# A hybrid decoder step on one core: state loads, weight splits, broadcast loads and a second half's operands in another order

## The chip, the core and the metric

The kernel runs on one core of a Trainium2 chip. The metric is device time in microseconds (us), from the start of the execution to its end; smaller is better. Engines are named as in the profile: PE is TensorE's matmul, DVE is VectorE, ACT is ScalarE, POOL is GpSimd, SP is SyncE, which here only issues DMAs.

## The reference

One layer of a decoder (model width 1024) for two groups that share the weights: a prompt of 1024 tokens and 8 samples of one token each, with carried states. All is float32.

```python
h = rmsnorm(x) * (1 + scale1) + shift1            # shift, scale, gate from the conditioning c
qkv, gate, beta, a, sq, sk, sv, ga, gb = split(h @ w_in)
y_a = (gated_rmsnorm(gated_delta_rule(conv4(qkv), beta, a)) ) @ w_gdn_out   # 8 heads, 128 x 128 state
y_b = sliding_window_attention_with_sinks(sq, sk, sv) @ w_swa_out
x   = x + gate1 * ((sigmoid(ga) * y_a + sigmoid(gb) * y_b) @ w_o)
h2  = rmsnorm(x) * (1 + scale2) + shift2
x   = x + gate2 * ((silu(causal_dwconv3(h2 @ w_ffn_gate)) * (h2 @ w_ffn_up)) @ w_ffn_down)
y   = rmsnorm(x)                                  # outputs: y and the new states of both groups
```

For the samples the delta rule is one step from a carried state S (8 samples, 8 heads, 128 x 128 floats: 512 KB a head): S' = exp(g) S + k delta, which is an output.

## The kernel before, in words

Every matmul operand in float32 is split in two parts of a shorter type: `split` (L127) lets ACT write the high part (`hi`, the page's L129) and DVE the low part `x - hi` (L130). A product is then three matmuls, hi hi, hi lo, lo hi (`mm3`, the page's L200, L201, L202). Tokens (1024 of the prompt and 8 samples) lie on the free axis in three `PARTS` of 384, 384 and 264; a weight of 1024 x 128 (512 KB) is loaded into `raw` and split into `wh` and `wl` by `load_split` (L147), which leaves the load in `self.w_load` and its two split instructions in `self.rounded`. `project_steps` (L167) gives 8 steps of three matmuls for one weight and one part.

What stands where in an engine's row is decided by a scheduler that simulates a timeline with priorities. `weave` (L1286) mixes several streams of steps by priority; `issue_after` says after which instruction another one is issued; `order(later, first)` (L132) puts instructions behind others of the same engine, without a wait. Each engine works its row in order, SP too: where a load waits for its buffer, all loads behind it wait.

The first half ends so:
- `delta_scan` (L946) runs the delta rule's chunks of the last head one after the other. A chunk is a chain of small steps: PE `rc` (L971), DVE `y` (L972), PE `rc` (L974), ACT `s` (L976), PE `rc` (L978), DVE the next `S` (L990). The last head's small DVE and ACT steps are kept in `self.small`, with the number of PE steps (`self.steps`) that had been recorded. `spaced` and `passed` (L181, L189) use them to spread the projections' matmuls and evictions between them: one PE step for every `self.every` = 2 projection steps, counted in `self.at`.
- `early_out` (L1332) is such a projection: the attention's output `ob` (kept in DRAM, laid in SBUF for parts 2 and 0) times the eight column blocks of `w_swa_out`, in `EARLY_ORDER` 0, 1, 2, 5, 6, 7, 3, 4; part 2 for all, part 0 also for blocks 3 and 4. Each result (`mm`) is multiplied by its gate tile (`gt`, loaded from `sgb` at L1353 into one of a few buffers) and goes to DRAM as `ub`. Here too the first six heads' sample states are loaded (`load_state`, L1144) into `b1h` and `b1l`.
- `branches` (L1363) does the rest of that product (part 1, loaded from `ob` into `b2l` in four quarters of 384 KB at L1278, and what is left of part 0), with the samples' delta rule (`sample_delta`, L1148) beside it, and then `y_a`: the delta rule's output `oa` times `w_gdn_out`, two blocks at a time. At the end of `sample_delta` each head's `delta` (in DRAM, `dlr`) is loaded as a broadcast into one of two halves of `db` (L1241, a `b1l` in the trace) and scaled with k by eight ACT instructions (L1243, `self.scaled`), then DVE forms the new state and POOL stores it.

The second half (`second_half`, L1959) is output projection, second norm and the FFN. `operands` (L1560) makes, of a half `p` of the tokens, seven combined operands (`ops[0]` to `ops[6]`, sums and differences of four quarters of x1), each split in hi and lo; stage 0 makes the first two, stage 1 the other five. For p = 1 their buffers are `bmh2, bml2, pk2, pk3, pk4, pk5, bmh3`. `pair_weights` (L1616) does the same to the FFN's weights (`w`, `ws`), and `ffn_gate_up` (L1693) runs the seven products of a pair (`wv`, `mm`, `wy` are their PSUM tiles) and recombines them on DVE and ACT.

Of the kernel before, what the change touches and what calls it, by code (L numbers as in the profile page):

```python
# [18 lines left out]
P = 128  # L19
NP = 1024  # L20
NS = 8
NT = NP + NS
KC = 8
H = 8
# [5 lines left out]
EARLY = (3, 4)  # L30
# [34 lines left out]
class Step:  # L65
# [1082 lines left out]
    def sample_delta(self, pool2):  # L1148

        nc, I = self.nc, self.I  # L1150
# [69 lines left out]
        dlr = self.t(self.dr, [H, NS, P], "dlr")  # L1220
# [16 lines left out]
        for h in range(H):  # L1237
            if h % 4 == 0:
                yield
            d = db[:, h % 2 * NP:h % 2 * NP + NP].rearrange("p (b v) -> p b v", b=NS)  # L1240
            nc.sync.dma_start(d, dlr[h].unsqueeze(0).broadcast_to([P, NS, P]))  # L1241
            for b in range(NS):
                made = nc.scalar.activation(d[:, b, :], d[:, b, :], AF.Copy, scale=kq[:, h, b, 0:1])  # L1243
                self.scaled.setdefault(h, []).append(made)
                nc.vector.scalar_tensor_tensor(S0[h][:, b, :], S0[h][:, b, :], self.egb[:, b, 0, h:h + 1], d[:, b, :],
                                               op0=ALU.mult, op1=ALU.add)
            nc.gpsimd.dma_start(self.O[3][0][:, h].rearrange("b k v -> k b v"), S0[h])
# [84 lines left out]
    def early_out(self):  # L1332

        nc = self.nc
        self.ubd = {t: self.t(self.dr, [8, P, PARTS[t][1]], f"ub{t}") for t in (2, 0)}
        load = lambda j: self.load_w(self.I["w_swa_out"][0][:, j * P:(j + 1) * P],
                                     where=self.fill_where[j % len(self.fill_where)])
        self.S0, states = [], [self.flat_room(self.b1, "b1", x, 1) for x in "hl"]
        X = {2: self.load_part(self.b1, self.ob, 2, "b1")}
        w = load(EARLY_ORDER[0])  # L1340
        for i, j in enumerate(EARLY_ORDER):
            if i == 3:
                self.obX = {0: self.load_part(self.b1, self.ob, 0, "b1")}
                X.update(self.obX)
            now, w = w, load(EARLY_ORDER[i + 1]) if i < 7 else None
            if i == 6:
                with self.tc.issue_after(self.w_load.ins):
                    for h in range(6):
                        self.load_state(h, states[h // 3])
            for t in (2, 0) if j in EARLY else (2,):  # L1350
                lo, n = PARTS[t]
                s = self.t(self.gt[0], [P, 384], self.gt[1])[:, :n]
                nc.sync.dma_start(s, self.sgb[j][:, lo:lo + n])  # L1353

                def out(t, ps):
                    with self.passed():
                        nc.vector.tensor_tensor(s, ps, s, op=ALU.mult)
                    nc.gpsimd.dma_start(self.ubd[t][j], s)

                for _ in self.project_steps(now, X, out, (t,), self.fill_psum):  # L1360
                    yield

    def branches(self, pool, pool2):  # L1363
        nc, I = self.nc, self.I
        first = self.part_rooms(pool2, 0)
        ob = {**self.obX, 1: self.load_part(pool2, self.ob, 1)}
        ub = [self.t(pool, [P, KC, n], f"t{t}", bufs=1) for t, (_, n) in enumerate(PARTS)]
        samples, rows, self.scaled = self.sample_delta(pool2), self.last_rows(), {}
        gate = lambda src, j, t: self.gate_part(pool if src is self.sga and j > 5 else self.gt[0], src[j][:, PARTS[t][0]:PARTS[t][0] + PARTS[t][1]], t)

        def yb_out(t, ps):
# [41 lines left out]
        for j0 in (0, 2, 4, 6):  # L1413
            w = []
            for j in (j0, j0 + 1):
                w.append(self.load_w(I["w_gdn_out"][0][:, j * P:(j + 1) * P]))
                for h in {1: range(3, H), 2: (6, 7)}.get(j, ()):
                    self.order(self.scaled[h], self.rounded)
            if 0 < j0 < 6:
                for j in (j0, j0 + 1):  # L1420
                    self.project(w[j - j0], oa, ya_out)
                continue

            for ts in ((0,), (2,), (1,)) if j0 == 0 else ((0,), (1,), (2,)):
                for j in (j0, j0 + 1):
                    self.project(w[j - j0], oa, ya_out, ts)
# [133 lines left out]
    def operands(self, pool, p, stage):  # L1560

        n = QUARTERS[2 * p][1]
        x1 = self.x1[p]
        a1, a2, b1, b2 = (x1[:, k:k + 4, c:c + n] for c in (0, n) for k in (0, 4))
        if stage == 0:
            self.X[p] = [(t[:, 0:4, :n], t[:, 4:8, :n]) for t in self.pair_tiles(p)]
        ops = self.X[p]
        if stage == 0:  # L1570
            self.split(*ops[0], a1)
            yield
            self.split(*ops[1], a2)
            yield
            return
        d = self.t(pool, [P, 4, QW], "td", bufs=1)[:, :, :n]
        minus = lambda out, x, y: self.nc.vector.tensor_tensor(out, x, y, op=ALU.subtract)
        minus(a1, b1, a1)
        self.split(*ops[3], a1)
        yield  # L1580
        minus(d, b2, a1)
        self.split(*ops[2], d)
        yield
        minus(b1, b2, b1)
        self.split(*ops[4], b1)
        yield
        minus(a2, a2, d)
        self.split(*ops[5], a2)
        yield
        self.split(*ops[6], b2)  # L1590
        yield


# [533 lines left out]
```

## Time and profile before

| | us |
|---|---|
| three runs | 2075.91, 2066.82, 2076.16 |
| their median | 2075.91 |
| profiled execution | 2069.76 |
| its span, first to last instruction | 2068.1 |
| PE busy | 2009.2 |
| DVE, ACT, POOL busy | 1356.6, 901.7, 525.0 |

The span is what the trace covers; the profiled execution is 1.7 us longer. Its mean granted TensorE clock is 0.990 of full speed. Times in the trace are counted from the span's start.

### The profile page before, as it was taken

The page shows a single profiled execution, that of the slowest core. Times are in us where ns is not written, and L with a number is a line of the kernel's source. Part 1 is how long each engine was busy: PE and PEld are TensorE (multiplying, and loading weights), DVE is VectorE, ACT ScalarE, POOL GpSimd, SP SyncE. Part 2 cuts the span into 40 slices and gives each one's busy share as a digit, 9 for nine tenths or more (in the row PEclk, how much of TensorE's full clock was granted, in tenths as well). Part 3 has the DMA queues.
Part 4 walks back from the last instruction along what each step waited for, and adds up shares of the span by engine and source line. Part 5 has one row for each costly group of instructions (what it writes and reads, how often), then busy time and mean ns, then how long its engine had stood idle before and what let it go on. Part 6 is the DMA issues. An engine that isn't in the chain of part 4 may idle for free.

```text
span 2068.1 us, 41309 instructions
## 1 busy us (share of the span) xinstructions
PE 2009.2 (97%) x16245; PEld 1909.6 (92%) x16245; DVE 1356.6 (66%) x2714; ACT 901.7 (44%) x2233; POOL 525.0 (25%) x604
## 2 busy tenths in 40 slices
PE   7999998999999999989999999999999999999998
PEld 4987877799999999989989999999999999999998
DVE  5755767483655746646554575579876777679876
ACT  4664545443344343442442352345544444445444
POOL 2000000121321211201112010104556556543551
PEclk9999999999999999989999999999999999999999
DMA  9256443332322322312248774522333333377783
GB/s 303 62 145 211 137 168 117 100 98 63 83 82 57 78 70 52 92 37 61 64 144 243 233 242 115 174 67 89 98 98 100 111 93 93 124 277 279 265 281 129
DMA packets 300960, 275.75 MB, mean 133 GB/s; under 512 B 59731, under 2 KB 246832, under 8 KB 300749
## 3 DMA queue, kind: packets, MB, share of 16 engines
q1 hardware_dynamic: 294202, 250.66, 39.7%
q0 software_dynamic: 6064, 21.85, 3.0%
q8 instruction: 127, 2.08, 0.4%
q14 instruction: 69, 0.56, 0.1%
q10 hardware_dynamic: 498, 0.61, 0.1%
HBM read 212.93 MB, written 62.51 MB: 133 GB/s over the span
## 4 chain that ended last, share of the span: by engine, by line
PE 85%; DVE 6%; DMA 4%; ACT 3%; issue 1%; SPq 0%; POOL 0%; ACTq 0%; DVEq 0%; POOLq 0%
PE mm L200 19%; PE mm L201 18%; PE mm L202 18%; PE wv L200 3%; PE wv L202 3%; PE wv L201 3%; PE wy L202 2%; PE wy L200 2%; PE wy L201 2%; PE pv L672 1%; DMA raw<-in_w_swa_out_dram 1%; PE pt L210 1%; PE tp L210 1%; PE mm L284 1%; PE rc L978 1%
## 5 line engine op out<-in xcount | busy, mean ns | idle before, releaser
L200 PE MATMUL mm<-b1h,wh 128*128 128x384 f32 (+1 forms) x1520 | 498.1, 329 | 3.4 <-ACT gt L1322 1.6
L201 PE MATMUL mm<-b1l,wh 128*128 128x384 f32 (+1 forms) x1520 | 489.9, 323 | 0.0
L202 PE MATMUL mm<-b1h,wl 128*128 128x384 f32 (+1 forms) x1520 | 488.6, 324 | 0.0
L200 PEld LDWEIGHTS mm<-b1h,wh 128*128 128x128 f32 x1520 | 287.6, 189 | 12.0 <-issue 4.6
L201 PEld LDWEIGHTS mm<-b1l,wh 128*128 128x128 f32 x1520 | 287.6, 189 | 4.4 <-issue 3.1
L202 PEld LDWEIGHTS mm<-b1h,wl 128*128 128x128 f32 x1520 | 286.6, 189 | 3.7 <-issue 2.8
L130 DVE TENSOR_TENSOR wl<-raw,wh 128x1024 fp32r<-128x1024 f32 x82 | 102.6, 1252 | 65.9 <-ACT wh L129 63.7
L129 ACT ACTIVATE wh<-raw 128x1024 fp32r<-128x1024 f32 x83 | 87.1, 1049 | 131.1 <-PE mm L201 80.0
L201 PE MATMUL mm<-pk,w 128*128 128x260 f32 (+1 forms) x440 | 124.7, 284 | 1.1 <-DVE pk L130 1.1
L200 PE MATMUL mm<-pk,w 128*128 128x260 f32 (+1 forms) x440 | 124.7, 284 | 0.0
L202 PE MATMUL mm<-pk,w 128*128 128x260 f32 (+1 forms) x440 | 124.5, 283 | 0.0
L130 DVE TENSOR_TENSOR w<-ws,w 128x512 fp32r<-128x512 f32 x88 | 78.8, 896 | 38.9 <-ACT w L129 38.7
L1666 ACT COPY bml<-mm 128x256 f32<-128x256 f32 (+1 forms) x132 | 49.0, 371 | 102.0 <-PE mm L202 99.4
L200 PE MATMUL mm<-bmh,w 128*128 128x260 f32 (+1 forms) x320 | 90.3, 282 | 0.0
L202 PE MATMUL mm<-bmh,w 128*128 128x260 f32 (+1 forms) x320 | 90.2, 282 | 0.0
L200 PE MATMUL mm<-b2h,wh 128*128 128x384 f32 (+1 forms) x256 | 83.3, 327 | 2.6 <-ACT wh L129 2.6
L1721 DVE SCALAR_TENSOR_TENSOR fa<-fz,fcw,fa 128x512 f32<-128x512 f32 x88 | 73.3, 854 | 18.4 <-ACT fa L1719 18.1
L201 PEld LDWEIGHTS mm<-pk,w 128*128 128x128 f32 x440 | 83.2, 189 | 1.3 <-DVE pk L130 1.3
L201 PE MATMUL mm<-b2l,wh 128*128 128x384 f32 (+1 forms) x256 | 83.6, 327 | 0.0
L200 PEld LDWEIGHTS mm<-pk,w 128*128 128x128 f32 x440 | 83.2, 189 | 0.2 <-ACT bml L1666 0.2
L202 PEld LDWEIGHTS mm<-pk,w 128*128 128x128 f32 x440 | 83.4, 190 | 0.0
L202 PE MATMUL mm<-b2h,wl 128*128 128x384 f32 (+1 forms) x256 | 82.6, 325 | 0.0
(648 smaller groups left out, 5886.7 us busy)
## 6 DMA issues: line engine op xcount, KB each, us to landing
raw<-in_w_in_dram SPq DMA_DIRECT2D x59, 512.0 KB
ws<-in_w_ffn_down_dram SPq DMA_DIRECT2D x55, 256.0 KB
raw<-xd SPq DMA_DIRECT2D x47, 258.0 KB
raw<-in_w_ffn_down_dram SPq DMA_DIRECT2D x47, 256.0 KB
raw<-in_w_ffn_gate_dram SPq DMA_DIRECT2D x22, 512.0 KB
raw<-in_w_ffn_up_dram SPq DMA_DIRECT2D x22, 512.0 KB
qst<-in_w_mod_dram SPq DMA_DIRECT2D x16, 512.0 KB
raw<-in_w_mod_dram SPq DMA_DIRECT2D x16, 512.0 KB
```

The source lines that it names most:

```text
L129: return (self.nc.scalar.activation(hi, x, AF.Copy), (eng or self.nc.vector).tensor_tensor(lo, x, hi.bitcast(F32), op=ALU.subtract))
L130: (eng or self.nc.vector).tensor_tensor(lo, x, hi.bitcast(F32), op=ALU.subtract))
L200: mm(ps, whi, xhi, start=first, stop=False, **kw)
L201: mm(ps, whi, xlo, start=False, stop=False, **kw)
L202: self.last_mm = mm(ps, wlo, xhi, start=False, stop=last, **kw).ins
L210: self.nc.tensor.transpose(out, in_, self.ident[:p, :p])
L284: nc.tensor.matmul(ps[32 * j:32 * j + 32], self.cT[:, k0 + j, :], ws[j // 2][:, j % 2, :], start=k0 == 0, stop=k0 > 0)
L672: nc.tensor.matmul(pv[64 * r:64 * r + 64], V[:, n - back, ch], ps[:, r::2, :], start=back == 0, stop=back == (n > 0))
L978: yield step(nc.tensor.matmul(ds, kd[:, n, :], s, start=True, stop=True))
L1666: self.last_copy = nc.scalar.copy(r[p, i], x[p])
L1721: nc.vector.scalar_tensor_tensor(ai[:, c:e], zi[:, j + c:j + e], col(j), ai[:, c:e], op0=ALU.mult, op1=ALU.add)
```

## The change

Four places get another order; what is computed, the instructions and their sizes stay.

1. `early_out`: the six state loads are no longer issued after the sixth block's weight load (i == 6), but after the very last gate load.
2. `early_out`: while the scan's steps are being spread, the split of the next weight is ordered behind up to four of the scan's small instructions, those that were recorded up to the present point and one step further.
3. `branches` and `sample_delta`: the broadcast loads of `dlr` (`self.spread`) of heads 2 and 3 are ordered behind the load of `w_gdn_out`'s block 1, those of heads 4 and 5 behind block 2's. The scaling instructions of heads 1 to 7 are ordered behind the split of block 0, of heads 2 to 7 behind block 1's (3 to 7 before), of heads 6 and 7 behind block 2's, as before.
4. `operands`, stage 1 of p = 1: the subtractions and splits of operands 4, 5 and 6 are ordered behind the split of operand 2.

```diff
@@ -1238,7 +1238,7 @@
             if h % 4 == 0:
                 yield
             d = db[:, h % 2 * NP:h % 2 * NP + NP].rearrange("p (b v) -> p b v", b=NS)
-            nc.sync.dma_start(d, dlr[h].unsqueeze(0).broadcast_to([P, NS, P]))
+            self.spread[h] = nc.sync.dma_start(d, dlr[h].unsqueeze(0).broadcast_to([P, NS, P]))
             for b in range(NS):
                 made = nc.scalar.activation(d[:, b, :], d[:, b, :], AF.Copy, scale=kq[:, h, b, 0:1])
                 self.scaled.setdefault(h, []).append(made)
@@ -1343,14 +1343,17 @@
                 self.obX = {0: self.load_part(self.b1, self.ob, 0, "b1")}
                 X.update(self.obX)
             now, w = w, load(EARLY_ORDER[i + 1]) if i < 7 else None
-            if i == 6:
-                with self.tc.issue_after(self.w_load.ins):
-                    for h in range(6):
-                        self.load_state(h, states[h // 3])
-            for t in (2, 0) if j in EARLY else (2,):
+            if w and self.steps:
+                self.order(self.rounded, [x for n, x in self.small if n <= self.at // self.every + 1][-4:])
+            ts = (2, 0) if j in EARLY else (2,)
+            for t in ts:
                 lo, n = PARTS[t]
                 s = self.t(self.gt[0], [P, 384], self.gt[1])[:, :n]
-                nc.sync.dma_start(s, self.sgb[j][:, lo:lo + n])
+                gate = nc.sync.dma_start(s, self.sgb[j][:, lo:lo + n])
+                if i == 7 and t == ts[-1]:
+                    with self.tc.issue_after(gate.ins):
+                        for h in range(6):
+                            self.load_state(h, states[h // 3])
 
                 def out(t, ps):
                     with self.passed():
@@ -1366,6 +1369,7 @@
         ob = {**self.obX, 1: self.load_part(pool2, self.ob, 1)}
         ub = [self.t(pool, [P, KC, n], f"t{t}", bufs=1) for t, (_, n) in enumerate(PARTS)]
         samples, rows, self.scaled = self.sample_delta(pool2), self.last_rows(), {}
+        self.spread = {}
         gate = lambda src, j, t: self.gate_part(pool if src is self.sga and j > 5 else self.gt[0], src[j][:, PARTS[t][0]:PARTS[t][0] + PARTS[t][1]], t)
 
         def yb_out(t, ps):
@@ -1414,8 +1418,10 @@
             w = []
             for j in (j0, j0 + 1):
                 w.append(self.load_w(I["w_gdn_out"][0][:, j * P:(j + 1) * P]))
-                for h in {1: range(3, H), 2: (6, 7)}.get(j, ()):
+                for h in {0: range(1, H), 1: range(2, H), 2: (6, 7)}.get(j, ()):
                     self.order(self.scaled[h], self.rounded)
+                for h in {1: (2, 3), 2: (4, 5)}.get(j, ()):
+                    self.order([self.spread[h]], [self.w_load])
             if 0 < j0 < 6:
                 for j in (j0, j0 + 1):
                     self.project(w[j - j0], oa, ya_out)
@@ -1579,15 +1585,15 @@
         self.split(*ops[3], a1)
         yield
         minus(d, b2, a1)
-        self.split(*ops[2], d)
+        made = self.split(*ops[2], d)
         yield
-        minus(b1, b2, b1)
-        self.split(*ops[4], b1)
+        rest = [minus(b1, b2, b1), *self.split(*ops[4], b1)]
         yield
-        minus(a2, a2, d)
-        self.split(*ops[5], a2)
+        rest += [minus(a2, a2, d), *self.split(*ops[5], a2)]
         yield
-        self.split(*ops[6], b2)
+        rest += self.split(*ops[6], b2)
+        if p:
+            self.order(rest, made)
         yield
```

The rows that follow are the engines' own, in the order in which they stand there; a name's number tells one tile from another.

**The scan's end.** ACT's row, near 1080 us of the trace before. `s_...` are the scan's small steps (L976), `wh_...` the high halves of `w_swa_out`'s blocks. Before:

```order
L129 ACTIVATE wh_12452<-raw_12450 128x1024
L129 ACTIVATE wh_12417<-raw_12415 128x1024
L976 ACTIVATE s_12263<-rc_12261,c_1909_11985 128x128
L976 ACTIVATE s_12276<-rc_12274,c_1909_11985 128x128
L129 ACTIVATE wh_12487<-raw_12485 128x1024
L976 ACTIVATE s_12290<-rc_12288,c_1909_11985 128x128
L129 ACTIVATE wh_12522<-raw_12520 128x1024
L976 ACTIVATE s_12304<-rc_12302,c_1909_11985 128x128
```

and in the changed kernel:

```order
L976 ACTIVATE s_12263<-rc_12261,c_1909_11985 128x128
L129 ACTIVATE wh_12417<-raw_12415 128x1024
L976 ACTIVATE s_12276<-rc_12274,c_1909_11985 128x128
L129 ACTIVATE wh_12452<-raw_12450 128x1024
L976 ACTIVATE s_12290<-rc_12288,c_1909_11985 128x128
L129 ACTIVATE wh_12487<-raw_12485 128x1024
L976 ACTIVATE s_12304<-rc_12302,c_1909_11985 128x128
L996 ACTIVATE osq_1977_12312,so_12258<-o_12260 128x128 x4
```

Each `s` now stands ahead of the weight split that stood ahead of it.

SP's row shortly after, about the states. `b1h`, `b1l` from `in_state_gdn_S` are the sample states, `gt` from `sgb` gate tiles (L1353 in `early_out`, now L1352; L1430 in `branches`, now L1436), `raw` weights, `b2l` from `ob` part 1. Before:

```order
L1146 DMA b1l_1876_11804<-in_state_gdn_S_dram 128x8x128 x3
L150 DMA raw_12685<-in_w_swa_out_dram 128x8x128
L1353 DMA gt_12532<-sgb_2613 128x264
L1353 DMA gt_12561<-sgb_2613 128x384
L1353 DMA gt_12590<-sgb_2613 128x264
L150 DMA raw_12691<-in_w_swa_out_dram 128x8x128
L1353 DMA gt_12619<-sgb_2613 128x384
L150 DMA raw_12805<-in_w_swa_out_dram 128x8x128
L1430 DMA gt_12730<-sgb_2613 128x384
L1146 DMA b1h_2051_12733<-in_state_gdn_S_dram 128x8x128 x2
L1430 DMA gt_12767<-sgb_2613 128x384
L1278 DMA b2l_2037_12669<-ob_380 128x2x384 x4
```

and now:

```order
L1352 DMA gt_12526<-sgb_2613 128x264
L1352 DMA gt_12555<-sgb_2613 128x384
L150 DMA raw_12685<-in_w_swa_out_dram 128x8x128
L1352 DMA gt_12584<-sgb_2613 128x264
L150 DMA raw_12691<-in_w_swa_out_dram 128x8x128
L1352 DMA gt_12613<-sgb_2613 128x384
L1146 DMA b1h_1875_11803<-in_state_gdn_S_dram 128x8x128 x3
L1146 DMA b1l_1876_11804<-in_state_gdn_S_dram 128x8x128 x3
L150 DMA raw_12805<-in_w_swa_out_dram 128x8x128
L1146 DMA b1h_2051_12733<-in_state_gdn_S_dram 128x8x128 x2
L1436 DMA gt_12730<-sgb_2613 128x384
L1278 DMA b2l_2037_12669<-ob_380 128x2x384 x4
```

All gate loads of `early_out` and the next three weights stand ahead of the states, whose eight loads now stand next to each other but for one weight, and right behind them the gate tile and the four quarters of part 1.

**Branches.** SP's row where `y_a` begins. `raw` from `in_w_gdn_out` are its blocks 0, 1 and 2, `b1l` from `dlr` the broadcasts, `b2l` from `oa` the operands. Before:

```order
L150 DMA raw_13464<-in_w_gdn_out_dram 128x8x128
L1278 DMA b2l_2110_13423<-oa_927 128x2x256 x2
L1430 DMA gt_13419<-sgb_2613 128x384
L1278 DMA b2l_2110_13423<-oa_927 128x2x256 x2
L1241 DMA b1l_2052_12734<-dlr_13089 128x1024
L1430 DMA gt_13501<-sga_2614 128x384
L1241 DMA b1l_2052_12734<-dlr_13089 128x1024
L150 DMA raw_13470<-in_w_gdn_out_dram 128x8x128
L1278 DMA b2l_2112_13439<-oa_927 128x2x384 x4
L1430 DMA gt_13534<-sga_2614 128x384
L1241 DMA b1l_2052_12734<-dlr_13089 128x1024
L1430 DMA gt_13567<-sga_2614 128x264
L150 DMA raw_13674<-in_w_gdn_out_dram 128x8x128
```

and now:

```order
L150 DMA raw_13464<-in_w_gdn_out_dram 128x8x128
L1278 DMA b2l_2110_13423<-oa_927 128x2x256 x2
L1436 DMA gt_13419<-sgb_2613 128x384
L1278 DMA b2l_2110_13423<-oa_927 128x2x256 x2
L1436 DMA gt_13501<-sga_2614 128x384
L150 DMA raw_13470<-in_w_gdn_out_dram 128x8x128
L1241 DMA b1l_2052_12734<-dlr_13089 128x1024
L1278 DMA b2l_2112_13439<-oa_927 128x2x384 x2
L1241 DMA b1l_2052_12734<-dlr_13089 128x1024
L1278 DMA b2l_2112_13439<-oa_927 128x2x384 x2
L1436 DMA gt_13534<-sga_2614 128x384
L1436 DMA gt_13567<-sga_2614 128x264
L150 DMA raw_13674<-in_w_gdn_out_dram 128x8x128
```

Block 1 (`raw_13470`) stood behind the broadcasts of heads 2 and 3, and now stands ahead of them; the others stand further behind. On ACT, block 0's split now stands behind eight scaling instructions and not sixteen, and block 1's behind sixteen and not twenty-four.

**Operands of the second half.** DVE's row, stage 1 for p = 1. `td` is the difference of which operand 2 (`pk_..._15500`) is split, `pk_..._15501` is operand 3, `15502` and `15503` are 4 and 5, `bmh_..._15504` is 6; L1577 (now L1583) are the subtractions, `w_...` low halves of FFN weights. Before:

```order
L1577 TENSOR_TENSOR x_2197_14334<-x_2197_14334 128x4x260
L130 TENSOR_TENSOR pk_2311_15501<-x_2197_14334,pk_2311_15501 128x1040
L1577 TENSOR_TENSOR x_2197_14334<-x_2197_14334,td_15571 128x4x260
L1709 TENSOR_TENSOR fz_15604<-wv_15651,bml_2334_15602 128x256
L130 TENSOR_TENSOR bmh_2314_15504<-x_2197_14334,bmh_2314_15504 128x1040
L130 TENSOR_TENSOR w_2368_16074<-raw_16069,w_2368_16074 128x512
L130 TENSOR_TENSOR pk_2310_15500<-td_15571,pk_2310_15500 128x1040
L130 TENSOR_TENSOR pk_2312_15502<-x_2197_14334,pk_2312_15502 128x1040
L1741 TENSOR_TENSOR bml_2334_15602<-wy_15883,bml_2334_15602 128x256
L130 TENSOR_TENSOR pk_2313_15503<-x_2197_14334,pk_2313_15503 128x1040
L130 TENSOR_TENSOR w_2353_15839<-ws_15832,w_2353_15839 128x512
```

and now:

```order
L130 TENSOR_TENSOR pk_2311_15501<-x_2197_14334,pk_2311_15501 128x1040
L1715 TENSOR_TENSOR fz_15604<-wv_15651,bml_2334_15602 128x256
L130 TENSOR_TENSOR w_2368_16074<-raw_16069,w_2368_16074 128x512
L130 TENSOR_TENSOR pk_2310_15500<-td_15571,pk_2310_15500 128x1040
L1583 TENSOR_TENSOR x_2197_14334<-x_2197_14334 128x4x260
L1583 TENSOR_TENSOR x_2197_14334<-x_2197_14334,td_15571 128x4x260
L130 TENSOR_TENSOR bmh_2314_15504<-x_2197_14334,bmh_2314_15504 128x1040
L1747 TENSOR_TENSOR bml_2334_15602<-wy_15883,bml_2334_15602 128x256
L130 TENSOR_TENSOR w_2353_15839<-ws_15832,w_2353_15839 128x512
L130 TENSOR_TENSOR pk_2312_15502<-x_2197_14334,pk_2312_15502 128x1040
L130 TENSOR_TENSOR w_2352_15836<-ws_15834,w_2352_15836 128x512
L130 TENSOR_TENSOR pk_2313_15503<-x_2197_14334,pk_2313_15503 128x1040
```

Operand 2's low half stood behind two subtractions and operand 6's low half, which now stand behind it.

## Rows read from the trace of the kernel before

**Rows 1.** The page: busy time and share of each engine; the chain that ended last, by engine.

```profile
PE 2009.2 (97%) x16245; PEld 1909.6 (92%) x16245; DVE 1356.6 (66%) x2714; ACT 901.7 (44%) x2233; POOL 525.0 (25%) x604
...
PE 85%; DVE 6%; DMA 4%; ACT 3%; issue 1%; SPq 0%; POOL 0%; ACTq 0%; DVEq 0%; POOLq 0%
```

**Rows 2.** PE's waits, 1040 to 1200 us: us in total, times, longest.

```profile
PE rc L978 <- ACT s L976: 2.7, 1, 2.7
PE mm L200 <- ACT wh L129: 2.6, 1, 2.6
PE rc L974 <- DVE y L972: 2.3, 2, 2.0
```

**Rows 3.** PE's waits, 1280 to 1440 us.

```profile
PE wv L200 <- ACT w L129: 1.1, 1, 1.1
PE mm L201 <- DVE pk L130: 1.1, 1, 1.1
...
PE wv L201 <- DVE pk L130: 0.3, 1, 0.3
```

**Rows 4.** Windows: length, busy PE, PEld, DVE, ACT, POOL, clock, DMA share, GB/s.

```profile
1080.00:1090.00 10.00, 7.26 (x48) 7.05 (x47) 4.00 (x6) 2.65 (x5) 0.54 (x1) 0.83 0.79 237
1090.00:1100.00 10.00, 10.00 (x85) 9.94 (x84) 5.93 (x13) 4.66 (x14) 1.08 (x2) 1.00 1.14 319
...
1110.00:1120.00 10.00, 10.00 (x64) 10.00 (x64) 3.58 (x8) 3.27 (x11) 2.64 (x4) 0.86 0.56 175
...
1190.00:1200.00 10.00, 7.35 (x41) 7.03 (x41) 6.57 (x18) 6.80 (x15) 1.48 (x2) 0.83 1.07 380
...
1405.00:1410.00 5.00, 3.92 (x20) 3.92 (x21) 4.74 (x6) 1.42 (x3) 0.00 (x0) 0.66 0.58 186
```

**Rows 5.** ACT's timeline, 1078 to 1090: start, length, instruction, idle before it.

```profile
1083.91 1.06 ACT L129 ACTIVATE wh<-raw 128x1024 fp32r<-128x1024 f32 x1 [2.52 <-DMA raw<-in_w_swa_out_dram]
1084.88 0.35 ACT L976 ACTIVATE s<-rc,c 128x128 f32<-128x128 f32 x1
```

**Rows 6.** SP's timeline, 1074 to 1132: start, time to issue, DMA, how many.

```profile
1077.78 0.39 SPq L150 DMA_DIRECT2D raw<-in_w_swa_out_dram  x1
...
1091.09 6.46 SPq L1146 DMA_DIRECT2D b1l<-in_state_gdn_S_dram  x3
...
1099.71 7.24 SPq L1353 DMA_DIRECT2D gt<-sgb  x3
...
1109.78 0.32 SPq L1353 DMA_DIRECT2D gt<-sgb  x1
...
1124.33 1.99 SPq L1278 DMA_DIRECT2D b2l<-ob  x4
```

**Rows 7.** DVE's timeline, 1104 to 1111.

```profile
1106.96 0.43 DVE L1357 TENSOR_TENSOR gt<-mm,gt 128x264 f32<-128x264 f32 x1 [2.31 <-DMA gt<-sgb]
1107.31 1.21 DVE L130 TENSOR_TENSOR wl<-raw,wh 128x1024 fp32r<-128x1024 f32 x1
...
1109.11 0.34 DVE L972 SCALAR_TENSOR_TENSOR y<-rc,d,vn 128x128 f32<-128x128 f32 x1
```

**Rows 8.** PE's timeline at four places.

```profile
1085.28 0.54 PE L978 MATMUL rc<-s,kd 128*128 128x128 f32 x2 [2.73 <-ACT s L976]
...
1089.31 0.38 PE L974 MATMUL rc<-y,W 128*128 128x128 f32 x2
...
1131.39 0.60 PE L200 MATMUL mm<-b2h,wh 128*128 128x384 f32 x2
...
1406.08 0.39 PE L201 MATMUL mm<-pk,w 128*128 128x260 f32 x1 [1.08 <-DVE pk L130]
```

**Rows 9.** SP's timeline, 1176 to 1196.

```profile
1186.10 0.38 SPq L150 DMA_DIRECT2D raw<-in_w_gdn_out_dram  x1
```

**Rows 10.** ACT's timeline, 1178 to 1196.

```profile
1188.12 2.45 ACT L1243 ACTIVATE b1l<-b1l,kq 128x128 f32<-128x128 f32 x8 [1.17 <-DMA b1l<-dlr]
1193.77 1.06 ACT L129 ACTIVATE wh<-raw 128x1024 fp32r<-128x1024 f32 x1 [3.19 <-DMA raw<-in_w_gdn_out_dram]
```

**Rows 11.** DVE's timeline, 1397 to 1412.

```profile
1404.79 1.23 DVE L130 TENSOR_TENSOR pk<-td,pk 128x1040 fp32r<-128x1040 f32 x1
```

## The prediction

> **What bounds the kernel now.** I began with the page's busy shares and its chain. TensorE is busy for 97% of the span and holds 85% of the chain that ended last; the rest of that chain is short pieces of DVE, DMA and ACT [rows 1]. So only what TensorE waits for counts, and what its clock does behind a wait. Next I read TensorE's waits in the two stretches that the change touches. In 1040–1200 us there are three waits of 2 us or more: 2.7 for the scan's `s`, 2.6 for a weight's `wh`, 2.0 for the scan's `y` [rows 2]. In 1280–1440 us there are two of 1.1, for a `w` split on ACT and for a `pk` split on DVE [rows 3]. Third came the windows, for the clock. The granted clock is 0.83 in 1080–1090, 0.86 in 1110–1120, 0.83 in 1190–1200 and 0.66 in the 5 us from 1405, and 1.00 between [rows 4]. A mean of 0.83 over 10 us is 3.4 us at the lower level, 1.2 GHz, in place of 2.4, each time behind one of these waits; lost are 10 × 0.17 = 1.7 us, 1.4, 1.7, and 5 × 0.34 = 1.7. Together 9.5 us of waits and 6.5 of half clock: 16.0 us is about the most that the change can reach in these places. (0.5%, some 10 us, is about what a measurement of this kernel can tell from no change.)
>
> **The change, place by place.** All of it is order: no instruction is added or dropped, so no term is an instruction's own duration. What counts is who stands behind whom.
>
> *Delta scan's end (1080–1131 us).* Three edits meet here: states later, the weight's splits behind the scan's small steps, and their consequences in SP's row.
>
> The first wait: `s` ran at 1084.88, directly behind a `wh` split of 1.06 us that itself had waited for its raw load [rows 5]. That load went out at 1077.78 and landed only at 1083.91, 6.1 us later [rows 5, 6]. With the change `s` stands ahead of both splits, and its operand was there: the wait of 2.7 and its 1.7 of half clock go. Late next is the same weight's low half: 1083.91 plus 1.06 plus a `wl` of 1.21 [rows 7] is 1086.2, and the scan's next `y` (0.34) stands behind that `wl` on DVE, so it ends at 1086.5. TensorE would come to it at about 1084.8: L978 at 1085.28 less 2.7 is 1082.6, and L974 follows it by 4.0 us in the trace, of which 1.7 is half clock [rows 8]. A new wait of 1.7.
>
> The second wait: `y` at 1109.11 stood behind a `wl` (1107.31) and an eviction at 1106.96 that waited 2.31 us for its gate tile [rows 7]. The gate's load is in a group issued from 1099.71 on, behind three states that alone held SP's queue for 6.46 us [rows 6]. In the new row that gate load goes out ahead of every state, so the 2.0 and the 1.4 behind it go. Left are waits of the sort that the new order makes: `s` behind the `wh` of a weight whose load now goes out two places later (I take 0.5; 0 if it lands early, 4 if it takes the 7.7 us of the load at 1186.10 [rows 9, 10]), and a `y` behind the fourth `wl` (0.5; 0 to its 1.2). Whether a wait of 1.7 takes the clock down no row tells: I take no, bounds 0 and 1.7. By the end of this stage 7.8 − (1.7 + 0.5 + 0.5) = 5.1 us are gained.
>
> Then part of it is given back. Eight states of 512 KB now stand right ahead of the four loads of `ob` part 1, that in the trace were issued at 1124.33; TensorE began on that part at 1131.39 [rows 6, 8] and would now come at 1126.3. The last gate load was at 1109.78 [rows 6]; with fewer stalls ahead, and no states, I put it and so the first state at 1106.6. Behind it come 4.2 MB of states, a weight (0.5), a gate (0.2), the first quarter of part 1 (0.4) and about 0.9 MB from POOL: 6.2 MB. While states moved in the trace the rate was 319 GB/s [rows 4], so 19.4 us: 1126.0, plus 1.9 for its two splits, 1127.9; I take 1128.5 for a little queueing. That is a wait of 2.2 that was not there, and I charge 0.7 of half clock for it (half of the 1.4 that the wait of 2.0 cost). So this place gives −5.1 + 2.2 + 0.7 = **−2.2 us**; bounds −5.1, if the part is there in time, and +2, if the load of `wh` takes 7.7 or the part comes 4 us later.
>
> The Trainium skill ("DMA: Bandwidth & Descriptors", Queues, rings and completion order) says that each DMA engine takes the descriptors of an issuing engine's ring in order; this speaks against the edit, since part 1 cannot overtake the states. The trace agrees as far as the gate load behind three states goes [rows 6, 7]. By that page's limit of about 358 GB/s from HBM to one core the quarter would land at 1123.9 (an estimate), and the place would give −5.1.
>
> *Loads and splits in the branches (1176–1200 us).* The weight whose `wh` ended the wait of 2.6 was issued at 1186.10 and landed at 1193.77 [rows 9, 10]; meanwhile ACT was free from 1190.6 on, behind eight scaling steps (2.45). In the new row that load stands ahead of two of the `dlr` broadcasts, and the previous weight's `wh` ahead of a head's eight steps, so the buffer it waits for is free a little earlier: I take 1185.2. If it then lands in 6.1 us, as the load at 1077.78 did, `wh` ends at 1192.4, 0.2 behind the 1192.2 (1194.8 less 2.6) at which TensorE wants it, and of 2.6 + 1.7 = 4.3 only 0.2 stay. If it takes 7.7 again, `wh` ends at 1194.0 and 0.9 is won. I take **−3.5**, nearer the first, since fewer loads stand ahead of it; bounds −4.3 and −0.5. The scaling steps and their loads only become later: their results (states of the sample) are stored, and nothing on TensorE waits for them.
>
> *Operands of the second half (1398–1432 us).* DVE works without a gap here. `pk` from `td` (operand 2's low half) ran at 1404.79, 1.23 long, so until 1406.0; TensorE wanted it at 1405.0 [rows 3, 11, 8]. Three of the steps that stood ahead of it, two subtractions and a low half at 1.15 us from start to start, now stand behind: 1402.6, and that wait and most of the clock's loss go. But DVE is as full as before, so what was moved back is late next: operand 4's high half waits on ACT for its subtraction, and behind it on ACT stands a weight's split that TensorE wants (I take 0.6), and the `w` low halves behind it (0.8); a bank or two besides (0.5). Of 1.1 + 1.1 + 1.7 = 3.9 I take −3.9 + 1.9 = −2.0, and 0.3 more for the small wait on `pk` [rows 3]: **−2.3**. Bounds −3.9, and +1.5 if one of the new waits takes the clock down in turn (1.7) and the row behind shifts by two operations of 1.15.
>
> **Sum.** −2.2 − 3.5 − 2.3 = −8.0 us. The profiled execution took 2069.76 us, and lies 6.15 under the median of the three runs, 2075.91. In its own terms the change gives 2061.8; against the median, **2067.9 us**.
>
> **Rivals.**
> - *The states make part 1 late* (the other side). One mechanism: eight states ahead of the `ob` loads. For it speaks that the rate was only 237 GB/s in 1080–1090 [rows 4], against it that this slice was half empty of requests. At 237 the 6.2 MB take 26.2 us: 1106.6 + 26.2 + 1.9 = 1134.7, or 1137.9 if the last gate load is at 1109.8 as before. It decides from 1137.2 on, where the loss of 5.8 against 1131.4 equals what the other two places give. At 1137.9 with 1.5 of half clock the sum is 6.5 + 1.5 − 5.8 = +2.2: 2078. Later still, at 1146, it would be 0.5% slower. 0.13, of it 0.05 beyond 0.5%.
> - *Waits only move.* Every moved step stays on a full engine: `y` behind `wl`, the weight's load 7.7 us as before, DVE full in the second half, each with its fall of the clock. For it: DVE's saturated stretch, and a new wait of 1.7 by my own replay. About −1: 2075. 0.17.
> - *All waits go.* Part 1 is there in time and the new waits come out at nothing: −7.8 − 4.3 − 3.9 = −16.0: 2060. Against it is the load of 1077.78 that no edit makes earlier. 0.15.
>
> **How the numbers follow.** Forecast 0.55, the three rivals 0.13, 0.17 and 0.15. The forecast's own range is −13 to −3, 2063 to 2073; some 2 in 5 of it lies beyond 10 us. Faster by over 0.5%: 0.22 from there, 0.14 from the third rival, 0.01 from the rest: 0.37. Slower by over 0.5%: 0.05 from the first rival and 0.01 from the forecast's tail: 0.06. The rest, 0.57, is within. The range takes in the third rival at the lower end (2060, and 2 us for the runs, which differ by 9 among themselves) and the first at 2078 with 2 us: 2058 to 2080.
>
> **What would show it.** Right: no wait of TensorE for `s` or `y` above 2 us in 1080–1115, all gate loads out before the first state; a new wait of about 2 us at the first matmul on `ob` part 1; no wait for `wh` near 1192; clock 1.00 in most of these windows; the waits near 1404 under 1 us. Wrong: a wait on part 1 above 6 us, a wait for `wh` of 2 us or more that merely stands elsewhere, or a clock still at 0.8 in the same slices; and a gain outside these three places, which I do not expect, since the other rows stand as they did.

## The result, and the profile after

| | before | changed |
|---|---|---|
| median of 22 runs each, us | 2069.22 (2064.44 to 2076.16) | 2073.02 (2068.87 to 2079.14) |
| span of the profiled execution, us | 2068.1 | 2069.6 |
| its mean granted clock | 0.990 | 0.993 |

The ratio of the changed kernel to the one before is 1.002, with a 95% interval of 1.0011 to 1.0028: some 4 us slower. The forecast was 8 us faster. The three runs of before that were known when it was made had a median of 2075.91, which was chance; over 22 runs before stands at 2069.22, near its profiled execution of 2069.76.

The page of the changed kernel: the span, the engines' busy times, the chain that ended last.

```profile
span 2069.6 us, 41304 instructions
...
PE 2007.6 (97%) x16245; PEld 1905.6 (92%) x16245; DVE 1350.7 (65%) x2714; ACT 901.4 (44%) x2233; POOL 525.0 (25%) x604
...
PE 84%; DVE 6%; DMA 4%; ACT 3%; issue 1%; SPq 1%; POOL 0%; DVEq 0%; POOLq 0%; ACTq 0%
```

Shares tell nothing here; they stand as before [rows 1]. The stages do. I took the start of the same row of PE in both timelines as a mark, and read the lengths between the marks:

| stage, from mark to mark (PE's timeline) | before | changed | difference | forecast |
|---|---|---|---|---|
| to the first `tp<-W` of the last inverse (L1101) | 1073.97 | 1072.32 | −1.65 | 0 |
| scan: to its last `o<-s` (L982; 1116.18, 1110.54) | 42.21 | 38.22 | −3.99 | −5.1 |
| part 1: to the sample step L1229 (1170.13, 1173.86) | 53.95 | 63.32 | +9.37 | +2.9 |
| rest of the branches: to `w_o` (L1476, now L1482; 1282.10, 1282.78) | 111.97 | 108.92 | −3.05 | −3.5 |
| output and norm: to L1545, now L1551 (1391.56, 1393.09) | 109.46 | 110.31 | +0.85 | 0 |
| second half: to the end | 676.54 | 676.51 | −0.03 | −2.3 |

The first row lies ahead of the waits that the edits aim at; over the thirteen traces of this document that mark lies anywhere from 1072.3 to 1077.7, so its difference is chance. The others sum to +3.15 us, which agrees with the measured 4. Two of the three gains that were forecast are there; what eats them is the stage of part 1.

PE's waits of the changed kernel, 1040 to 1210 us (us in total, times, longest):

```profile
PE mm L1173 <- DVE b2h L1165: 5.6, 1, 5.6
PE rc L974 <- DVE y L972: 3.0, 3, 2.2
PE mm L200 <- DVE gt L1360: 0.7, 1, 0.7
```

The waits for `s` and for `wh` [rows 2] are gone, and a new one of 5.6 us is larger than either. The windows (columns as in [rows 4]) show what stands behind it:

```profile
1080.00:1090.00 10.00, 7.80 (x53) 7.60 (x52) 5.02 (x9) 2.74 (x4) 1.08 (x2) 0.83 0.61 196
...
1110.00:1120.00 10.00, 10.00 (x66) 9.96 (x64) 2.42 (x7) 1.63 (x9) 3.24 (x5) 1.00 1.14 305
1120.00:1130.00 10.00, 5.36 (x29) 4.71 (x28) 1.96 (x5) 0.37 (x1) 2.23 (x4) 1.00 1.12 343
1130.00:1140.00 10.00, 7.98 (x31) 7.40 (x32) 5.26 (x10) 3.38 (x4) 1.22 (x1) 0.66 0.55 192
...
1190.00:1200.00 10.00, 10.00 (x62) 10.00 (x61) 9.22 (x21) 6.46 (x14) 1.77 (x2) 1.00 1.00 320
...
1395.00:1445.00 50.00, 45.87 (x363) 43.75 (x363) 47.37 (x67) 27.98 (x52) 22.40 (x22) 1.00 0.25 78
```

The clock is full at 1110–1120 and at 1190–1200, where it was 0.86 and 0.83; in 1130–1140, behind the new wait, it is 0.66, which is another 3.4 us lost (some of it while PE still waited). The whole stage of part 1, before and changed:

```profile
1116.18:1170.13 53.95, 53.48 (x422) 51.90 (x420) 25.56 (x53) 15.38 (x28) 6.75 (x10) 1.00 0.69 210
1110.54:1173.86 63.32, 56.66 (x421) 54.24 (x419) 25.95 (x53) 15.47 (x28) 6.69 (x10) 0.95 0.75 226
```

PE is idle for 6.7 us of it (63.32 − 56.66: 5.6, the 0.7 for `gt`, and 0.4 for `b2h`, below), where it was idle for 0.5. These 6.2 us, and some 3.2 us of half clock (63.32 × 0.05), are the 9.4 of the stage.

Where the 5.6 come from is read backwards. PE's, ACT's and DVE's timelines:

```profile
1131.60 0.59 PE L1173 MATMUL mm<-ones,b2h 128*128 128x1 f32 x2 [5.58 <-DVE b2h L1165]
1132.61 1.01 PE L200 MATMUL mm<-b2h,wh 128*128 128x384 f32 x2 [0.43 <-ACT b2h L129]
```

```profile
1131.72 2.74 ACT L129 ACTIVATE b2h<-b2l 128x768 fp32r<-128x768 f32 x3 [9.60 <-DMA b2l<-ob]
```

```profile
1130.79 0.56 DVE L1376 TENSOR_TENSOR t<-mm,gt 128x384 f32<-128x384 f32 x1 [8.28 <-DMA gt<-sgb]
1131.26 0.28 DVE L1165 TENSOR_TENSOR b2h<-b2h 128x128 f32<-128x128 f32 x1
```

PE waits for a small DVE step (L1165) that stands behind an eviction (L1376), and that eviction has waited 8.28 us for its gate tile. One microsecond later the first quarter of part 1 lands, and PE has to wait 0.43 for its split. The gate tile and part 1 were both late, and it is the later of them that decides. SP's timeline says more:

```profile
1106.61 0.32 SPq L1352 DMA_DIRECT2D gt<-sgb  x1
1107.03 2.38 SPq L1146 DMA_DIRECT2D b1h<-in_state_gdn_S_dram  x3
1109.45 6.18 SPq L1146 DMA_DIRECT2D b1l<-in_state_gdn_S_dram  x3
1115.73 2.74 SPq L150 DMA_DIRECT2D raw<-in_w_swa_out_dram  x1
1118.57 4.36 SPq L1146 DMA_DIRECT2D b1h<-in_state_gdn_S_dram  x2
1123.02 2.07 SPq L1436 DMA_DIRECT2D gt<-sgb  x1
1125.14 3.09 SPq L1278 DMA_DIRECT2D b2l<-ob  x4
```

From 1107.03 to 1125.09 SP is issuing the eight states, a weight and the gate tile; part 1's loads go out at 1125.14, 0.8 us later than before [rows 6] though PE is 5.6 us ahead by the mark at L982. They land later, too: the first quarter 6.6 us behind its issue (1131.72), where before it took at most 4.2 (its split ran at 1128.48). The gate tile went out 16 us behind the first state and landed 7.8 us after that.

### The profile page after: what moved, and what is told of

It reads as the page before. It is cut to its first block, busy times and chain, and to the rows that moved or that the text cites. A ratio compares the mean times of both kernels' runs of the same rounds, so it can differ in the third digit from the quotient of the medians.

```text
span 2069.6 us, 41304 instructions
## 1 busy us (share of the span) xinstructions
PE 2007.6 (97%) x16245; PEld 1905.6 (92%) x16245; DVE 1350.7 (65%) x2714; ACT 901.4 (44%) x2233; POOL 525.0 (25%) x604
## 4 chain that ended last, share of the span: by engine, by line
PE 84%; DVE 6%; DMA 4%; ACT 3%; issue 1%; SPq 1%; POOL 0%; DVEq 0%; POOLq 0%; ACTq 0%
PE mm L200 18%; PE mm L201 18%; PE mm L202 18%; PE wv L200 3%; PE wv L202 3%; PE wv L201 3%; PE wy L202 2%; PE wy L200 2%; PE wy L201 2%; PE pv L672 1%; DMA b1l<-dlr 1%; PE pt L210 1%; PE tp L210 1%; PE mm L284 1%; PE sc L634 1%
```

## The experiments

All times are ratios to the kernel before, run on the same chip. Edits are numbered as in the section on the change. The lengths of the stages, from each run's PE timeline by the marks above, come from one profiled execution each, which need not lie near the run's median: that of operands_alone took 2073.3 us (median 2068.8), that of half_states 2068.4 (2063.7), that of last_no_operands 2067.9 (2062.7). Three runs have the scan in the same order (before, branches_alone, operands_alone), and there it took 41.7 to 43.3. So a difference of 1 us in a stage says nothing by itself.

| run | ratio (95%) | scan | part 1 | branches | output | second half |
|---|---|---|---|---|---|---|
| before | | 42.2 | 54.0 | 112.0 | 109.5 | 676.5 |
| changed | 1.002 (1.0011–1.0028) | 38.2 | 63.3 | 108.9 | 110.3 | 676.5 |
| states_alone (1) | 1.0015 (1.0001–1.0028) | 40.0 | 61.9 | 109.5 | 109.5 | 676.5 |
| scan_alone (2) | 1.0003 (0.9993–1.0013) | 45.1 | 53.9 | 111.7 | 109.5 | 675.6 |
| branches_alone (3) | 0.9997 (0.9983–1.0011) | 41.7 | 53.9 | 108.7 | 110.0 | 677.6 |
| operands_alone (4) | 0.9994 (0.9984–1.0005) | 43.3 | 54.0 | 112.4 | 109.6 | 677.8 |
| states_undone (2, 3, 4) | 1.0005 (0.9994–1.0015) | 44.6 | 53.9 | 109.1 | 109.4 | 676.5 |
| states_last | 0.9968 (0.9957–0.998) | 36.3 | 56.2 | 109.5 | 109.4 | 677.0 |
| half_states | 0.9982 (0.9971–0.9993) | 35.8 | 56.9 | 109.8 | 109.5 | 677.1 |
| split_states | 1.0028 (1.0018–1.0039) | 38.0 | 63.7 | 110.2 | 111.6 | 677.1 |
| part1_act | 1.0008 (0.9996–1.0019) | 36.1 | 62.4 | 108.9 | 109.6 | 677.5 |
| last_block2 | 0.9976 (0.9964–0.9988) | 40.1 | 56.1 | 108.9 | 109.2 | 676.8 |
| last_no_operands | 0.997 (0.9956–0.9985) | 36.6 | 56.8 | 111.4 | 109.3 | 676.3 |

**Edit 1 alone** (against before):

```diff
-            if i == 6:
-                with self.tc.issue_after(self.w_load.ins):
-                    for h in range(6):
-                        self.load_state(h, states[h // 3])
...
+                gate = nc.sync.dma_start(s, self.sgb[j][:, lo:lo + n])
+                if i == 7 and t == ts[-1]:
+                    with self.tc.issue_after(gate.ins):
+                        for h in range(6):
+                            self.load_state(h, states[h // 3])
```

> Edit 1 alone: the kernel before with the six state loads behind the last gate load. Theory A (the run of eight states ahead of the gate tile and part 1 of ob is what costs): the wait of 2.0 us for y near 1107 is gone, the wait of 2.7 for s stays, and TensorE waits 4 us or more at the first matmul that needs part 1 or its gate tile, with the clock near 0.7 in the next 10 us; 3 to 7 us slower than before. Theory B (the loss is made by the other edits, in the splits and the second half): no wait above 2.5 us there, and 1 to 4 us faster than before.

Its waits, 1070 to 1450, and one window:

```profile
PE mm L1173 <- DVE b2h L1165: 4.1, 1, 4.1
PE rc L978 <- ACT s L976: 3.5, 2, 3.3
```

```profile
1130.00:1140.00 10.00, 7.14 (x22) 6.56 (x23) 5.61 (x11) 3.38 (x4) 1.21 (x1) 0.66 0.63 225
```

The wait and the half clock are there with edit 1 and nothing else, and the stage of part 1 is 7.9 us longer; the wait for `s` stays, that for `y` is gone. This is theory A. (A ratio of 1.0015 is 3 us; the scan gave back 2.2 of the 7.9, and the branches 2.5, where a wait for `wh` of 1.8 happened to leave the clock up.)

**Edit 1 taken back** (against the changed kernel): the diff above, reversed.

> The changed kernel with edit 1 taken back: the states are issued at i == 6 again, edits 2 to 4 stay. Theory A: the wait of 5.6 us at the first step behind part 1 is gone, a wait of 2 to 3 us for a gate tile's eviction near 1107 is back; 2 to 6 us faster than before. Theory B: as slow as the changed kernel, 2 to 5 us slower than before.

The wait of 5.6 is gone and part 1 takes 53.9 again; the run is 3 us below the changed kernel, as theory A asks. The wait for a gate tile's eviction near 1107, which I expected back, is not there. And the run is not faster than before, since the scan is now the longest of all but one, 44.6. Its waits:

```profile
PE mm L200 <- ACT wh L129: 3.4, 1, 3.4
PE rc L974 <- DVE y L972: 2.5, 2, 1.5
```

With the states at their old place a weight's load stands behind them in SP's row (issued at 1096.40, behind six states issued from 1086.41 on), and its `wh` is 3.4 us late. **Edit 2 alone** shows the same (its diff is the two lines `if w and self.steps: self.order(...)`):

> Edit 2 alone. Theory A: the wait of 2.7 us for s goes, a wait of 1 to 2 us for y behind a weight's low half comes, the wait of 2.0 for y behind the gate tile stays (the states stand ahead of the gate loads); within 3 us of before, either way. Rival: it loses all of what it gains, 1 us slower or more.

The scan took 45.1, 2.9 us longer: waits for `wh` (2.2 of them in the scan) and `y` take the place of the one for `s`. The wait for `y` behind the gate tile, which theory A kept, is gone here as well: both waits for `y` (2.0 and 1.0) come behind a `wl`. By its ratio the run cannot be told from no change. So in these traces edit 2 costs 2 to 3 us in its stage without edit 1, and edit 1 gains 2.2 in the scan without edit 2; together they gain 4.0. Against the 1.6 us by which equal scans differ that is a clear sign, but no exact price; neither edit can be judged alone.

**The states behind part 1** (against the changed kernel):

```diff
-                if i == 7 and t == ts[-1]:
-                    with self.tc.issue_after(gate.ins):
-                        for h in range(6):
-                            self.load_state(h, states[h // 3])
...
         ob = {**self.obX, 1: self.load_part(pool2, self.ob, 1)}
+        with self.tc.issue_after(self.part_load.ins):
+            for h in range(6):
+                self.load_state(h, self.states[h // 3])
```

(`part_load` is the last load that `load_part` issued.)

> The changed kernel with the six state loads issued behind the four loads of ob part 1. Theory A: TensorE waits under 1 us at the first matmuls on part 1, and the clock stays at 1.00 between 1120 and 1140; 5 to 10 us faster than before, unless the sample step that reads the states (L1199) now waits, in which case a wait there shows what is late next. Theory B: no faster than before.

SP's timeline of this run, and its windows at the place:

```profile
1117.78 1.98 SPq L1278 DMA_DIRECT2D b2l<-ob  x4
1119.81 7.50 SPq L1146 DMA_DIRECT2D b1h<-in_state_gdn_S_dram  x3
1127.35 5.16 SPq L1146 DMA_DIRECT2D b1l<-in_state_gdn_S_dram  x3
```

```profile
1120.00:1130.00 10.00, 9.53 (x56) 9.47 (x56) 6.91 (x14) 3.53 (x5) 3.26 (x5) 1.00 1.05 322
1130.00:1140.00 10.00, 10.00 (x110) 9.24 (x109) 3.74 (x11) 1.58 (x3) 0.00 (x0) 1.00 1.18 304
```

These are the same six loads, behind nine others of the row that stood behind them, and PE loses no clock there and waits only 0.5 us, for an eviction (L1375) that it waited for before as well. The ratio of 0.9968 is 6.6 us faster than before, better than both kernels. The states come in while PE works on part 1. Part 1's stage is still 2.2 us above before; waits of 0.80 for a `wh` and 0.29 for its `wl` explain half of it, the rest I did not find.

**What of the states costs: bytes or loads?** Three runs on the changed kernel. Half of each of the six states left out:

```diff
-        self.nc.sync.dma_start(self.S0[h], self.I["state_gdn_S"][0][:, h].rearrange("b k v -> k b v"))
+        n = NS // 2 if h < 6 else NS
+        self.nc.sync.dma_start(self.S0[h][:, :n], self.I["state_gdn_S"][0][:n, h].rearrange("b k v -> k b v"))
+        if n < NS:
+            self.nc.gpsimd.memset(self.S0[h][:, n:], 0.0)
```

> The changed kernel, with only half of each of the six states loaded (256 KB in place of 512; the other half is set to zero, so the samples' delta rule is computed from other data). Theory C (the bytes ahead of part 1 decide): 1.6 MB less, at about 250 GB/s some 6 us, so the wait of 5.6 us for part 1 goes, and with it the half clock behind it; 6 to 10 us faster than the changed kernel. Theory D (the number of loads in flight decides, since each of the four loads of part 1 is issued only when a state load has landed): part 1's loads go out only a little earlier, and 3 us or more of the wait stay.

Each of the six in two loads:

```diff
+        for b in range(0, NS, NS // 2 if h < 6 else NS):
+            e = b + (NS // 2 if h < 6 else NS)
+            self.nc.sync.dma_start(self.S0[h][:, b:e], self.I["state_gdn_S"][0][b:e, h].rearrange("b k v -> k b v"))
```

> The changed kernel, with each of the six states loaded in two loads of 256 KB, so that the same bytes stand ahead of part 1 in twice as many loads. Theory C (bytes): the first quarter of part 1 lands at the same time as in the changed kernel, the wait behind it stays at 4 to 6 us and the time within 2 us of the changed kernel. Theory D (the number of loads): part 1's loads are issued or land 3 us or more later, a wait of 8 us or more, and some 3 to 5 us slower than the changed kernel.

Here is, for these two, the first state's issue (SP) and the first quarter's split (ACT), half_states first:

```profile
1110.41 1.48 SPq L1147 DMA_DIRECT2D b1h<-in_state_gdn_S_dram  x3
...
1130.16 0.84 ACT L129 ACTIVATE b2h<-b2l 128x768 fp32r<-128x768 f32 x1 [3.08 <-DMA b2l<-ob]
```

```profile
1109.10 3.63 SPq L1148 DMA_DIRECT2D b1h<-in_state_gdn_S_dram  x6
...
1133.95 0.84 ACT L129 ACTIVATE b2h<-b2l 128x768 fp32r<-128x768 f32 x1 [9.92 <-DMA b2l<-ob]
```

From the first state to part 1 it took 24.7 us in the changed kernel (1107.03 to 1131.72), 24.9 with twice the loads and the same bytes, 19.8 with 1.6 MB less. That is theory C, the bytes. In just these stretches the traces have moved 7.77, 7.79 and 6.35 MB, at 315, 313 and 321 GB/s: one rate, and the time goes with the bytes. The wait of 5.6 is gone in half_states (1.0 for the split and 1.7 for a gate tile remain, at full clock), and it is 8 us faster than the changed kernel (0.9982 against 1.002). The wait is 5.9 in split_states, whose 1.0028 lies within 2 us of the changed kernel's 1.002.

Last, part 1 and its gate tile issued by ACT:

```diff
-        ob = {**self.obX, 1: self.load_part(pool2, self.ob, 1)}
+        ob = {**self.obX, 1: self.load_part(pool2, self.ob, 1, eng=nc.scalar)}
+        self.first_gate = nc.scalar
```

> The changed kernel, with the four loads of ob part 1 and the gate tile ahead of them issued by ACT in place of SP, so that they stand behind no state in SP's row. If the place in SP's row decides (theory D, or a queue that is worked in order): part 1 lands in time, the wait of 5.6 us falls under 1 us, 6 to 9 us faster than the changed kernel. If the shared transfer rate decides (theory C): they share the rate with the states, land 2 to 4 us earlier than in the changed kernel, and 1 to 4 us of the wait stay.

ACT's timeline:

```profile
1113.05 0.36 ACTq L1437 DMA_DIRECT2D gt<-sgb  x1
1113.75 14.90 ACTq L1278 DMA_DIRECT2D b2l<-ob  x4
1128.70 0.36 ACT L1157 ACTIVATE b2h<-b2h 128x192 f32<-128x192 f32 x1 [17.74 <-DMA raw<-in_w_swa_out_dram]
```

This run is inconclusive for what it was meant to tell, though it shows something else. The gate tile, issued by ACT, was there for the eviction at 1120.07, at most 7 us after its issue and 14.8 after the first state's (1105.30). From SP's row it landed 7.8 us after its issue, but 23.8 after the first state's: what its place in SP's row cost it was mostly a later issue. The four loads of part 1 took 14.9 us to issue from ACT, against 3.1 from SP's row. What held them back the trace does not name; for SP it names an earlier load's landing once in this stretch (a gate load, L1437, waited 1.8 us for a `b1h` state). ACT stood there, and the small step L1157 behind them held up L1165 as the gate tile did in the changed kernel: 5.5 us. The place in the row was changed, and the wait only changed its reason.

**Edit 3 alone** (its three lines of the diff in front):

> Edit 3 alone. By the prediction's term: the wait of 2.6 us for wh near 1192 and its half clock go, 3.5 us faster than before. From the trace of the changed kernel: a wait of 1.3 to 1.5 us for a wl on DVE near 1210 comes in its place, without a fall of the clock, so 2 to 3 us faster. Rival: nothing gained.

```profile
PE mm L202 <- DVE wl L130: 1.0, 1, 1.0
```

That is what stands in the branches now, in place of 2.6 for `wh` and 1.7 of clock; the stage is 3.3 us shorter. The ratio, 0.9997 with an interval of 0.14% to each side, can hardly show 3 us. The column of the table shows the limits of this gain: the stage takes 108.7 to 110.2 in eight traces with edit 3, but 111.4 in the ninth (last_no_operands), where a wait for `wl` of 1.4 did take the clock down (0.83 in 1210–1220); and 111.7 to 112.4 in three traces without it, but 109.5 in the fourth (states_alone), where the clock stayed up.

**Edit 4 alone**:

> Edit 4 alone. By the prediction's term 2.3 us faster than before, with the waits near 1404 under 1 us. By a rival reading (DVE has no gap between 1395 and 1440, so any order of the same steps ends at the same time and the waits only move) within 1 us of before, with waits for other DVE results between 1404 and 1440 of the same sum, 3 to 4 us.

Its window, and that of the kernel before, over the whole place:

```profile
1395.00:1445.00 50.00, 45.91 (x364) 43.80 (x363) 47.59 (x66) 27.83 (x52) 21.84 (x22) 1.00 0.25 75
```

```profile
1395.00:1445.00 50.00, 46.45 (x368) 45.42 (x367) 47.65 (x66) 27.05 (x51) 24.41 (x24) 0.97 0.29 85
```

PE is idle for 4.1 us with edit 4 (50 − 45.91); without it for 3.6, and 1.5 of clock are lost besides (50 × 0.03): 4.1 against 5.1. In scan_alone, without edit 4, the clock stayed up and PE was idle for 3.3. The rival reading was nearer: the waits move, and what is won is the clock, when it would have fallen. (It fell, to 0.97, in four of the five traces without edit 4, and in none of the eight with it; but the second half as a whole took 675.6 to 677.6 without the edit and 676.5 to 677.8 with it, so no gain is left at its end.) **Edit 4 taken back from the best version**:

> The version with the states behind part 1, with edit 4 taken back. By the prediction's term for edit 4: 2.3 us slower than that version (ratio about 0.998). If edit 4 only moves the waits of the second half: within 1 us of it, with the waits near 1400 of before (1.1, 1.1, 0.3) in place of 0.7, 0.6, 0.9 and 1.3.

The ratios, 0.997 against 0.9968, do not differ, and the second half took 676.3 against 677.0. The waits of before (1.1, 1.1, 0.3) are back, as the second reading has it.

**One step further** (against states_last: `2: (6, 7)` becomes `2: range(4, H)` in the order of the scaling):

> The version with the states behind part 1, and besides the scaling of heads 4 and 5 ordered behind the split of block 2 of w_gdn_out (before only heads 6 and 7). If the wait of 1.5 us for a wl near 1209 comes from the sixteen scaling steps that stand ahead of that block's wh on ACT: it falls under 0.5, and the time is 1 to 2 us below that of the states behind part 1 (ratio 0.9957 to 0.9965). If DVE's own work ahead of the wl makes it: the wait stays above 1 us and nothing is gained.

The wait of 1.5 for a `wl` fell to 0.3, as the first theory has it, but waits for `wh` of 0.8 came twice, and the scan of this execution lost 3.0 for `y` and clock behind it. The ratio is 0.9976, whose interval overlaps that of states_last: nothing was gained that can be measured.

## Why the prediction was wrong

The mechanisms were nearly all found; one of them was far too cheap in the sum. Of the signs that the prediction named, some spoke against it: a wait for `y` of more than 2 us, the clock still at 0.83 in 1080–1090, and on part 1 a wait of 5.6 + 0.4, about the 6 us that it gave as the limit.

- **Part 1, the step that failed.** "Behind it come ... 6.2 MB", at 319 GB/s 19.4 us, so "a wait of 2.2", and "0.7 of half clock". The stage cost 9.4 in place of 2.9. The rate was right. The trace of the changed kernel, 1107 to 1132 us, which is from the first state to part 1 (all transfers, then SP's queue q1 and POOL's q0: packets, MB, share of the DMA engines):

```profile
DMA packets 10978, 7.88 MB, mean 315 GB/s; under 512 B 332, under 2 KB 10609, under 8 KB 10977
...
q1 hardware_dynamic: 10497, 6.35, 90.3%
q0 software_dynamic: 480, 1.51, 16.8%
```

The bytes were wrong: 7.8 to 7.9 MB and not 6.2, since POOL moved 1.5 and not 0.9, and since the quarters behind the first share the transfer with it: ACT splits the first three of them back to back from 1131.72 on, without a wait for the others (above). So it took 24.7 us and not 19.4. The start was 2.1 us later than assumed (1107.03, or 1108.7 in the time of before, whose mark lies 1.65 later), with the longer scan; but PE came to part 1 later by nearly as much (1128.3 in the time of before, in place of 1126.3), so this hardly counts. The split of the first quarter took less than assumed, 0.9 in place of 2.5. Together the wait was 6.0 and not 2.2. And the half clock was charged at 0.7, half of a short wait's 1.4; it was some 3.2 to 3.4, behind a wait more than twice as long.
- **The rival "the states make part 1 late"** is what happened: it put PE's start on part 1 at 1134.7, and it was at 1132.61, 1134.3 in the time of before. That the time fits is luck: the rival took 6.2 MB at 237 GB/s, and it was 7.8 MB at 315. I had it decide "from 1137.2 on", because it was weighed against 5.8 us of gains elsewhere; with 3.1 there, and 3.4 of half clock behind it, it decides from about 1131 on. The Trainium skill ("DMA: Bandwidth & Descriptors", Queues, rings and completion order) says that each DMA engine takes the descriptors of a ring in order, though loads need not complete in that order. The runs agree as far as they go: part 1, issued behind the states, landed 24.7 us after the first of them; but they do not tell order in the ring from the later issue. The page's figure of 358 GB/s was not reached in this stretch (315); elsewhere the core moved more ([rows 4]: 380 in 1190–1200).
- **Scan.** Right in kind: the `s` and the gate's `y` no longer wait, and `y` behind the weight's low half does. "A new wait of 1.7" was 2.19 and took the clock down (0.83 in 1080–1090), so it was −4.0 in place of −5.1. That edits 1 and 2 only pay together the prediction did not see.
- **Branches.** It was −3.05 for −3.5: mechanism and size right in this execution, with a wait of 1.27 for a `wl` near 1216 as the new one, which left the clock up. In last_no_operands the like wait did not, and the stage was only 0.6 us shorter than before; that the sum could count on 3.5 is not shown.
- **Second half.** It was −0.03 for −2.3. The sum left out a third wait of the place (1.0 for `bml`, L1741); with it, 5.1 us were lost in 1395–1445 before, and 4.1 with the change, so 1.0 was won there, and it is gone again at the end of the stage. DVE is as full as before, as the text said; the new waits, for the results of later steps on DVE and ACT, were priced at half (1.9 for 3.6):

```profile
PE mm L200 <- DVE fa L1749: 2.3, 2, 1.3
PE mm L200 <- DVE x L1517: 1.4, 2, 0.8
PE mm L200 <- ACT bml L1672: 0.7, 1, 0.7
PE wv L200 <- DVE fz L1715: 0.6, 1, 0.6
```

(1280 to 1440 us; the 1.4 lie ahead of the place, in the output pass, where they were 0.8 before: most of that stage's +0.85.)
- **The level.** 2067.9 was counted from a median of three runs that lay 6.7 us above that of 22; that brought the number nearer to the measured one than the reasoning was, by luck.

## What to carry to other kernels

Large loads that nobody needs soon belong behind the last load that the bound engine is about to ask for, not ahead of it: here the stage of part 1 took 9.4 us more with the six loads at one place in the row, and 2.2 more with them nine loads later. When a run of loads is moved, add up every byte that moves between its start and the next needed tile, of all queues, and of the loads issued right behind that tile too. And where an engine works without a gap, as DVE does in the second half here, another order of its work moved the waits and did not remove them: look for what is late next before counting a gain.

## What the hardware showed that was not expected

The price of a wait is not fixed by its length. A wait of 2.73 us near 1085 (before) and one of 2.19 (changed) were followed by a clock at 1.2 GHz for about 3.4 us; a wait of 2.68 at the same place in operands_alone was not (1.00 in 1080–1090), nor one of 2.04 near 1086 in scan_alone. A wait of only 1.40 was, near 1212 in last_no_operands (0.83 in 1210–1220). So a stage of one and the same order of work can differ by 1.7 us between executions, and a single profile over- or underprices a wait by as much.
